# Late index queries placed directly behind the first key/value products, and the second half's norm written columns first

## The chip, the cores and the metric

The kernel runs on one core of a Trainium2 chip. The metric is device time in microseconds (us) of one execution, as the median of several runs. A core has five engines with a queue of their own each: PE (matrix products and transposes, results in PSUM), DVE (vector work), ACT (scalar functions, copies, casts), POOL (a second elementwise engine) and SP (issues most DMAs). Each engine runs its queue in order and waits where an operand or a buffer isn't ready.

## The reference, cut to what matters

Two layers run over 528 tokens (16 meta tokens and 512 of the sequence), each with

```python
h = rms_norm(x, norm_g)
proj = jnp.einsum('btd,de->bte', h, w_in)
q, k, v, gate_a, u_b, gate_b, q_idx, k_idx, w_idx, merge = jnp.split(proj, ...)
k = apply_rope(rms_norm(k, kn_g), cos, sin)
q_idx = apply_rope(q_idx.reshape(B, T, N_IDX_HEADS, IDX_DIM), cos_h, sin_h)
k_idx = apply_rope(k_idx, cos, sin)
...
s = jnp.einsum('bqhd,bkd->bqhk', q_idx, k_idx)
score = jnp.einsum('bqhk,bqh->bqk', jax.nn.relu(s), w_idx * idx_scale)
_, sel = lax.top_k(score, k_top)
```

The index scores choose which keys each query attends to. Attention over the chosen keys, a pooling branch, two gates and an output product follow; they are not touched here.

## The kernel before, in words

**Tokens and halves.** The tokens lie in five groups t = 0 to 4 (`TOK`): the 16 meta tokens, then four of 128. The first half of the columns holds t = 0, 1, 2 (272 tokens), the second half t = 3, 4 (256). The normed input is kept three times: `nf` (float32), and split into `hhi` and `hlo`, a high and a low part for products in a faster format.

**Who orders what.** PE and DVE run in exactly the order in which the program writes their instructions. ACT, POOL and SP are ordered by the framework's scheduler; `tc.issue_after(ins)` keeps instructions of such an engine behind `ins`. `later(fn, n)` puts a piece of work behind the n-th next call of `group_done()`; each product group (some 3 us of PE) ends in one `group_done()`, which runs what is due, then one piece of weight preparation (`prep_one`), then takes one or two steps from `fill`, the list of index score steps. Below, "#n" is the n-th `group_done()` of a layer.

**The start of a layer** (lines 1172 to 1225) is where the change lies. On PE, in this order:
- `plain_trio`: keys, values and index keys of t = 1, 2 and, by columns, t = 0, from float32 `nf` and the raw weights. In layer 1 it has `stats(1)` inside, which sums the squares of the second half; POOL then makes `msq`, the factors of its norm. In layer 0 `x_half(1)` follows. #1 runs `kv_post` of t = 1 and 2 (rotary reads of PSUM on DVE).
- layer 1 only: `hooks[1]`, the second half's norm, `norm_half(1, 1, mm, LAG3)`.
- `late_queries(0)` (line 710): index queries of the 64 last tokens of t = 1, 32 small products into one bank `d`. Its `post`, which reads the bank on DVE with the rotary tables (`late_tab`), is due at #2.
- layer 0 only: the second half's norm, `norm_half(0, 1, rstd, LAG1)`. Then #2.
- index queries of t = 2 (`index_queries`, "q2", weights in split form); #3.
- keys and values of t = 3 ("k3") and of t = 4 ("k4") from `nf` of the second half, `plain_group`; #4 and #5.
- index queries of t = 3 ("q3") and 4 ("q4"); #6 and #7. Then the second set of weights: late queries, q2, q3, q4; #8 to #11.

`norm_half` (line 473) spreads the factors over the partitions by PE transposes into `rb`, then runs over k = 0 to 7: DVE writes column k of `nf` (a scalar_tensor_tensor that reads `rb` in PSUM), ACT copies it to `hhi`, and the low part `hlo` of column k - lag is taken (a tensor_sub of two SBUF operands, on POOL for k = 1, 3, 5, 7, on DVE for the others). The lag is 2 in layer 0 and 3 in layer 1, so columns and low parts alternate on DVE.

**PSUM.** Product groups use banks `d`, of which there are three: the trio takes two, the late queries the third, q2, k3 and k4 the same three again. A group can start when the DVE reads of the group three before it have ended. Transposes and scores use the four banks `a`.

**Behind the groups.** `kv_post` goes on with `second` (scaling), `third` (split into `ks`) and `trans` (PE transposes to the key tables `KK` and `KI`, copied by ACT): for t = 1, 2 at #2, #3, #5; for t = 0, whose sum ends at #2, at #3, #4, #6. The late queries: cast, subtraction, transposes and the entry of their two score steps into `fill` at #3, #5, #6 and #7. The score steps multiply with `KI[:, :, :144]`, that is with the index keys of t = 0 and 1.

**Rows turned out, layer 1.** `turn_rows(k)` transposes a tile of the layer's input on DVE into `turned` (four slots) and writes it to DRAM at the next `group_done()` in four SP DMAs (`kept<-turned`, line 1160). The eight calls stand in the first eight groups from #2 on. `turned` shares its memory (tag "D") with `silb`, which is written first behind the first gate product (`dense`, some 6 us behind q4 of the second set).

**Weights.** `w_prep_enqueue(True, after)` behind #5 enqueues the second index weights: two ACT casts (`w<-raw`, line 189) and two DVE subtractions. In layer 0 the casts are kept behind the norm's last `hhi` copy (`halved`); in layer 1 `after` is None. The next chunk (chunk 3) gets its low parts by an accumulating DMA from POOL (line 204).

Of the kernel before, what the change touches and what calls it, by code (L numbers as in the profile page):

```python
# [16 lines left out]
KT = D // 128  # L17
# [15 lines left out]
CAP = 1.5  # L33
W0 = 16
LAG0 = 2
LAG1 = 2
LAG2 = 3
LAG3 = 3
FI = 6
QN = 2  # L40
R_IDX = 3
# [47 lines left out]
def tile_block(ctx: ExitStack, tc: tile.TileContext, x, meta, w_in, pool_w, w_a, w_b, w_out, rows, hgain, c_tab, out):  # L89
# [43 lines left out]
    raws, ready = {}, {}  # L133
# [179 lines left out]
    def later(fn, n=2):  # L313
        pend.append((count[0] + n, fn))
# [159 lines left out]
    def norm_half(l, hf, rstd, lag=1, pool=(1, 3, 5, 7)):  # L474
        a, n = (0, HB) if hf == 0 else (HB, T - HB)
        rb = bank("a")
        for t in ((0, 1, 2) if hf == 0 else (3, 4)):
            s, m = TOK[t]
            pe.transpose(rb[:, s - a:s - a + m], rstd[:m, t:t + 1].to_broadcast([m, 128]), ident[:m, :m])
        if hf == 0:  # L480
            NF[0] = [one.tile([128, 4, T], F32, tag=tag, name="nf") for tag in ("Ahi", "Alo")]
        nf = [NF[0][k // 4][:, k % 4, a:a + n] for k in range(KT)]
        for k in range(KT + lag):
            if k < KT:
                t = nf[k]
                dve.scalar_tensor_tensor(t, RES[0][:, k, a:a + n], parT[:, l * 8 + k:l * 8 + k + 1], rb[:, :n],
                                         op0=OP.mult, op1=OP.mult)
                end = act.copy(hhi[:, k, a:a + n], t)
            if k >= lag:
                j = k - lag  # L490
                (gp if j in pool else dve).tensor_sub(hlo[:, j, a:a + n], nf[j], f(hhi[:, j, a:a + n]))
        return end.ins
# [214 lines left out]
        act.activation(X0["abs"], wp[:, :4], AF.Abs, scale=IDX_SCALE)  # L707
        act.activation(X0["sign"], wp[:, :4], AF.Sign, scale=-1.0)

    def late_queries(g, raw):  # L710
        ps = bank("d")
        for k in range(KT):
            for a in range(2):
                pe.matmul(ps[64 * a:64 * a + 64, :128], NF[0][k // 4][:, k % 4, 80:144],
                          raw[k // 4][:, k % 4, 128 * a:128 * a + 128], start=k == 0, stop=k == KT - 1,
                          skip_group_check=True)

        def post():
            p3 = ps[:, :128].rearrange("p (h d) -> p h d", h=2)
            t1 = tmp.tile([128, HB], F32, tag="tt", name="t1", bufs=6)  # L720
            t2 = tmp.tile([128, HB], F32, tag="tt", name="t2", bufs=6)
            v1 = t1[:, :128].rearrange("p (h d) -> p h d", h=2)
            dve.tensor_tensor(v1, p3, ctab0[:, None, :].to_broadcast([128, 2, 64]), op=OP.mult)
            dve.tensor_tensor(t2[:, :128].rearrange("p (h a d) -> p h a d", h=2, a=2), swapped(ps[:, :128], 2),
                              stab0.rearrange("p (a d) -> p a d", a=2)[:, None, :, :].to_broadcast([128, 2, 2, 32]),
                              op=OP.mult)
            gp.tensor_tensor(t1[:, :128], t1[:, :128], t2[:, :128], op=OP.add)
            qs = tmp.tile([128, 2, 128], F32R, tag="P", name="qs", bufs=PB)
            dst = tmp.tile([128, 2, 128], F32R, tag="B", name="q0", bufs=8)

            def trans():
                tp = bank("a", F32R)
                for b in range(2):
                    pe.transpose(tp[:, b * 128:b * 128 + 128], qs[:, b, :], identr)
                act.copy(dst, f(tp)[:, :256].rearrange("p (h c) -> p h c", h=2))
            later(lambda: act.copy(qs[:, :, 0:64], v1), 1)
            later(lambda: dve.tensor_sub(qs[:, :, 64:128], v1, f(qs[:, :, 0:64])), QI)
            later(trans, QI + 1)
            later(lambda: fill.append(late_scores(g, dst)), FI - 1)
        later(post, 1)  # L740

    def late_scores(g, q):
        n = NK[0]
# [397 lines left out]
    hooks = {0: lambda: None}  # L1141

    for l in range(2):
# [38 lines left out]
            later(lambda t=t, ps=pss[t]: kv_post(l, t, ps), 1)  # L1182
        later(lambda ps=pss[0]: meta_sum(ps, KV, lambda total: kv_post(l, 0, total)), 1)
        group_done()
        if l:
            hooks[1]()
        turns = deque(range(KT))

        def late_chunk(g, c):
            late_queries(g, raws.pop(c))  # L1190
            w_load()

        for what, t in (("q", 1), ("q", 2), ("k", 3), ("k", 4), ("q", 3), ("q", 4)):
            if what == "k":
                ps = plain_group(t, raws[kv])
                later(lambda t=t, ps=ps: kv_post(l, t, ps), 1)
            elif t == 1:
                late_chunk(0, early_raw)
                if l == 0:
                    halved = norm_half(0, 1, rstd, LAG1)  # L1200
            else:
                index_queries(t, 0, w)
            if l and turns:
                turn_rows(turns.popleft())
            group_done()
            if (what, t) == ("k", 4):
                del raws[kv]
                w_load()
                w_prep_enqueue(True, None if l else halved)
        w = chunk()  # L1210
        for t in range(1, 5):
            if t == 1:
# [185 lines left out]
        if l == 0:  # L1398
# [42 lines left out]
            for hs in (halves[:1], halves[1:]):  # L1441
# [5 lines left out]
                if hs[0][0] == 0:  # L1447
                    later(lambda: stats(0), 1)
                    later(lambda: norm_half(1, 0, mm, LAG2), 2)
            hooks = {0: lambda: stats(1), 1: lambda: norm_half(1, 1, mm, LAG3)}  # L1450
        else:
            for c in range(4):
                w = chunk()
# [66 lines left out]
```

## Time and profile before

| | |
|---|---|
| runs | 751.58, 752.74, 753.07 us; median 752.74 |
| profiled execution | 751.12 us, its span 749.3 us |
| granted TensorE clock | 0.998 |
| PE busy | 98% of the span |
| DVE, ACT, POOL busy | 76%, 62%, 28% |

The span runs from the first to the last instruction of the core; the execution's time is 1.8 us longer. A row of the timeline gives start, length, engine, line, operation, output and inputs, the number of instructions merged, and in brackets how long the engine sat idle before and what ended that. Nearly all PE and DVE instructions carry line 61, a helper, so they are told apart by their tiles. Layer 0 spans some 10 to 384 us, layer 1 the rest; the stretches in question are 18 to 45 us and 385 to 440 us.

### The profile page before, as it was taken

Reading aid. Unit: us, or ns where it says so; the run is one execution under the profiler, and the core shown is the slowest. Engines: PE = TensorE matmul, PEld = TensorE weight load, DVE = VectorE, ACT = ScalarE, POOL = GpSimd, SP = SyncE. Lnnn points to the kernel's source line nnn. Section 1 sums busy time; section 2 is a strip of 40 time slices with the busy share of each in tenths; the row PEclk is TensorE's granted clock in tenths of the full one; section 3 lists DMA queues with packets and bytes.
Section 4 is the critical chain, followed back from the end, with each engine's and each line's share of the span. In section 5 each row is a group of like instructions: output and inputs, shape, how many; then the busy total and the mean of one; then the engine's idle time right before and its main releaser. Section 6 shows DMA issues by size and latency. Waiting matters only on the chain.

```text
span 749.3 us, 15627 instructions
## 1 busy us (share of the span) xinstructions
PE 733.2 (98%) x5906; PEld 699.5 (93%) x5906; DVE 566.1 (76%) x1420; ACT 461.9 (62%) x1027; POOL 210.7 (28%) x280
## 2 busy tenths in 40 slices
PE   8999999999999999999998999999999999999998
PEld 7899999999999999999997988988989999999998
DVE  6866897789898776794448859987998878778631
ACT  5678745648878795543235688455587887774310
POOL 2651065243012010063345411761511110104200
PEclk9999999999999999999999999999999999999999
DMA  8658676776132222543404989768822332237321
GB/s 265 220 140 205 147 156 169 169 185 156 29 85 57 58 58 83 178 156 95 113 1 101 199 171 261 184 141 201 203 76 57 87 85 57 57 103 236 106 77 44
DMA packets 89003, 96.87 MB, mean 129 GB/s; under 512 B 20656, under 2 KB 75728, under 8 KB 88928
## 3 DMA queue, kind: packets, MB, share of 16 engines
q1 hardware_dynamic: 82800, 74.76, 33.6%
q0 software_dynamic: 5760, 20.97, 15.4%
q8 instruction: 46, 0.75, 0.4%
q14 instruction: 29, 0.24, 0.1%
q10 hardware_dynamic: 368, 0.15, 0.1%
HBM read 66.41 MB, written 8.49 MB: 100 GB/s over the span
## 4 chain that ended last, share of the span: by engine, by line
PE 81%; DVE 8%; ACT 8%; issue 2%; POOL 1%; DMA 1%; ACTq 0%; DVEq 0%; SPq 0%
PE d L61 69%; PE a L61 9%; PE v L61 3%; DVE w L61 2%; ACT lt L829 2%; ACT w L238 1%; ACT lt L840 1%; DVE raw L61 1%; DVE lt L61 1%; DVE c L61 1%; ACT pt L856 1%; DMA raw<-in_w_in_dram 1%; DVE alo L61 1%; DVE s L61 1%; DVE hlo L61 0%
## 5 line engine op out<-in xcount | busy, mean ns | idle before, releaser
L61 PE MATMUL d<-hhi,w 128*128 128x256 f32 (+3 forms) x1408 | 287.0, 296 | 0.2
L61 PEld LDWEIGHTS d<-hhi,w 128*128 128x128 f32 x1408 | 225.8, 188 | 5.9 <-DVE c L61 0.7
L61 PE MATMUL d<-hlo,w 128*128 128x256 f32 (+3 forms) x704 | 193.4, 294 | 0.0
L61 PEld LDWEIGHTS d<-hlo,w 128*128 128x128 f32 x704 | 132.8, 189 | 2.6 <-issue 0.2
L61 DVE TENSOR_TENSOR w<-raw,w 128x512 fp32r<-128x512 f32 (+1 forms) x128 | 107.8, 852 | 2.4 <-ACT w L238 2.3
L61 PE MATMUL d<-w,hhi 128*128 128x256 f32 x704 | 109.1, 284 | 0.0
L61 PEld LDWEIGHTS d<-w,hhi 128*128 128x128 f32 x704 | 96.0, 188 | 4.1 <-issue 1.8
L61 PE MATMUL d<-hsum,w 128*128 128x264 f32 (+1 forms) x576 | 76.5, 285 | 0.0
L841 POOL TENSOR_SCALAR pm<-lt,rs 128x16 f32<-128x16 f32 x48 | 27.8, 592 | 171.0 <-DVE rs L61 163.6
L61 PEld LDWEIGHTS d<-hsum,w 128*128 128x128 f32 x576 | 71.6, 188 | 0.8 <-ACT lt L840 0.3
L61 PE MATMUL d<-w,hlo 128*128 128x256 f32 x352 | 67.3, 281 | 0.0
L204 POOL DMA_DIRECT2D w<-raw x40 | 36.1, 916 | 100.2 <-ACT w L203 86.8
L238 ACT CAST w<-raw 128x512 fp32r<-128x512 f32 x96 | 56.9, 624 | 1.8 <-DVE raw L61 1.7
L1384 POOL TENSOR_TENSOR hlo<-ta,hhi 128x256 fp32r<-128x256 f32 (+1 forms) x28 | 28.2, 1020 | 96.5 <-PE d L61 83.2
L61 DVE MATCH_REPLACE8 sc<-m,sc 128x400 f32<-128x400 f32 (+2 forms) x100 | 54.3, 548 | 0.0
L61 DVE MAX8 m<-sc 128x8 f32<-128x400 f32 (+2 forms) x100 | 52.7, 556 | 0.8
L61 PEld LDWEIGHTS d<-w,hlo 128*128 128x128 f32 x352 | 52.7, 188 | 0.0
L829 ACT ACTIVATE lt<-lt,mn,NR 128x144 f32<-128x144 f32 (+3 forms) x64 | 42.4, 666 | 13.9 <-DVE mn L61 13.8
L61 PE MATMUL d<-mhi,w 128*128 128x272 f32 (+2 forms) x192 | 47.6, 328 | 0.0
L189 ACT CAST w<-raw 128x1024 fp32r<-128x1024 f32 x32 | 33.5, 1046 | 21.7 <-PE d L61 19.3
L203 ACT ACTIVATE w<-raw 128x1024 fp32r<-128x1024 f32 x40 | 41.5, 1059 | 7.0 <-PE d L61 7.0
L208 ACT CAST w<-raw 128x1024 fp32r<-128x1024 f32 x40 | 41.5, 1050 | 0.0
(224 smaller groups left out, 1386.6 us busy)
## 6 DMA issues: line engine op xcount, KB each, us to landing
raw<-in_w_in_dram SPq DMA_DIRECT2D x72, 512.0 KB, 4.3
w<-raw POOLq DMA_DIRECT2D x40, 512.0 KB, 6.0
raw<-in_w_out_dram SPq DMA_DIRECT2D x16, 512.0 KB, 3.5
raw<-in_w_branch_b_dram SPq DMA_DIRECT2D x8, 512.0 KB, 4.6
raw<-in_w_branch_a_dram SPq DMA_DIRECT2D x8, 512.0 KB, 4.0
kept<-res SPq DMA_DIRECT2D x8, 264.0 KB, 5.5
res<-kept SPq DMA_DIRECT2D x8, 264.0 KB, 5.7
xt<-in_x_dram SPq DMA_DIRECT2D x4, 512.0 KB, 6.1
```

The source lines that it names most:

```text
L61: return fn(*a, **k)
L189: act.copy(his[s], raws[c][s])
L203: act.activation(t, raws[c][s], AF.Copy, scale=-1.0)
L204: gp.dma_start(t, raws[c][s], accum_op=OP.add)
L208: act.copy(t, raws[c][s])
L238: act.copy(t[:, 0], blk[src[n]])
L829: act.activation(L[hh][:, :n], L[hh][:, :n], AF.Exp, scale=NR[:, i, h:h + 1], bias=mn[:, hh:hh + 1], accum_out=sm[:, hh:hh + 1])
L840: act.activation(L[hh][:, 16:n], L[hh][:, 16:n], AF.Copy, scale=rs[:, hh:hh + 1])
L841: (gp if j < 3 else dve).tensor_scalar(pms[i][:, 2 * j + hh, :], L[hh][:, 0:16], rs[:, hh:hh + 1], None, op0=OP.mult)
L856: act.copy(pt[:, :2 * len(bs)], tp[:, :256 * len(bs)].rearrange("p (a c) -> p a c", c=128))
L1384: pool_end = gp.tensor_sub(hlo[:, j, a:a + n], d, f(hhi[:, j, a:a + n]))
```

## The change

`late_queries` gets a flag `now`: its `post` then runs at once instead of at #2, so that all its later steps come one group earlier (cast #2, subtraction #4, transposes #5, entry into `fill` #6). In both layers the late queries stand directly behind #1, their rotary reads behind them, and the second half's norm behind those; the norm's lag is KT = 8, so that all eight columns come ahead of all eight low parts. In layer 1 the high casts of the second index weights are now kept behind the norm's last copy, too. `turn_rows` begins at k3: four calls at k3, k4, q3 and q4, four in the second set (#8 to #11).

```diff
-LAG1 = 2
...
-LAG3 = 3
...
-    def late_queries(g, raw):
+    def late_queries(g, raw, now):
...
-        later(post, 1)
+        if now:
+            post()
+        else:
+            later(post, 1)
...
-        if l:
-            hooks[1]()
         turns = deque(range(KT))

-        def late_chunk(g, c):
-            late_queries(g, raws.pop(c))
+        def late_chunk(g, c, now=False):
+            late_queries(g, raws.pop(c), now)
             w_load()

-        for what, t in (("q", 1), ("q", 2), ("k", 3), ("k", 4), ("q", 3), ("q", 4)):
+        late_chunk(0, early_raw, True)
+        halved = norm_half(0, 1, rstd, KT) if l == 0 else hooks[1]()
+        group_done()
+        for what, t in (("q", 2), ("k", 3), ("k", 4), ("q", 3), ("q", 4)):
             if what == "k":
                 ps = plain_group(t, raws[kv])
                 later(lambda t=t, ps=ps: kv_post(l, t, ps), 1)
-            elif t == 1:
-                late_chunk(0, early_raw)
-                if l == 0:
-                    halved = norm_half(0, 1, rstd, LAG1)
             else:
                 index_queries(t, 0, w)
-            if l and turns:
+            if l and t > 2:
                 turn_rows(turns.popleft())
             group_done()
             if (what, t) == ("k", 4):
                 del raws[kv]
                 w_load()
-                w_prep_enqueue(True, None if l else halved)
+                w_prep_enqueue(True, halved)
...
-            hooks = {0: lambda: stats(1), 1: lambda: norm_half(1, 1, mm, LAG3)}
+            hooks = {0: lambda: stats(1), 1: lambda: norm_half(1, 1, mm, KT)}
```

## The prediction, as written before the result

> **What bounds the kernel now.** I read the page first, then the waits of PE.
>
> ```profile
> span 749.3 us, 15627 instructions
> PE 733.2 (98%) x5906; PEld 699.5 (93%) x5906; DVE 566.1 (76%) x1420; ACT 461.9 (62%) x1027; POOL 210.7 (28%) x280
> ```
>
> ```profile
> PE d L61 <- DVE t L61: 3.5, 2, 2.2
> ...
> PE a L61 <- POOL msq L466: 1.1, 1, 1.1
> ```
>
> PE is busy 733.2 of 749.3 us, so 16 us is all that a reordering could win, and the change removes no product. What counts is which idle stretches of PE it touches. The second view names them (total, times, longest): two waits of PE for DVE's `t`, 3.5 us together, and one for POOL's `msq`. The timeline shows where they lie. First layer 0:
>
> ```profile
> 20.96 1.97 PE L61 MATMUL d<-raw,nf 128*64 128x128 f32 x32
> ...
> 23.33 1.26 DVE L61 SCALAR_TENSOR_TENSOR nf<-res,parT,a 128x256 f32<-128x256 f32 x3 [0.81 <-PE a L61]
> ...
> 25.43 1.43 POOL L491 TENSOR_TENSOR hlo<-nf,hhi 128x256 fp32r<-128x256 f32 x2
> ...
> 25.75 1.40 DVE L61 TENSOR_TENSOR hlo<-nf,hhi 128x256 fp32r<-128x256 f32 x1
> 26.82 2.87 PE L61 MATMUL d<-raw,nf 128*128 128x200 f32 x16
> ...
> 28.58 0.56 DVE L61 TENSOR_TENSOR hlo<-nf,hhi 128x256 fp32r<-128x256 f32 x1
> ...
> 30.39 0.47 DVE L61 TENSOR_TENSOR t<-d,late_tab 128x128 f32<-128x128 f32 x2
> ...
> 31.01 2.94 PE L61 MATMUL d<-raw,nf 128*128 128x200 f32 x16 [1.32 <-DVE t L61]
> ```
>
> The late queries (20.96, 32 products) end at 22.93. Their rotary reads run only at 30.39 to 30.86, behind the whole norm (23.33 to 29.14) on DVE. k3 (26.82) ends at 29.69; k4 needs the bank that the late queries still hold, and starts at 31.01, 1.32 us later. Layer 1 in the same view:
>
> ```profile
> 392.89 0.88 PE L61 MATMUL v<-raw,nf 128*32 128x200 f32 x16
> ...
> 394.92 0.43 PE L61 MATMUL a<-consts,msq 128*128 128x128 f32 x2 [1.14 <-POOL msq L466]
> ...
> 395.28 1.97 PE L61 MATMUL d<-raw,nf 128*64 128x128 f32 x32
> ...
> 397.69 1.21 PE L61 MATMUL d<-w,hhi 128*128 128x256 f32 x8
> ...
> 400.63 2.87 PE L61 MATMUL d<-raw,nf 128*128 128x200 f32 x16
> 400.96 1.05 ACT L189 CAST w<-raw 128x1024 fp32r<-128x1024 f32 x1 [1.95 <-DMA raw<-in_w_in_dram]
> ...
> 402.96 0.75 DVE L61 TENSOR_TENSOR hlo<-nf,hhi 128x256 fp32r<-128x256 f32 x1 [0.19 <-ACT hhi L488]
> ...
> 405.08 0.47 DVE L61 TENSOR_TENSOR t<-d,late_tab 128x128 f32<-128x128 f32 x2
> 405.69 2.94 PE L61 MATMUL d<-raw,nf 128*128 128x200 f32 x16 [2.19 <-DVE t L61]
> ```
>
> Two waits here. PE ends the trio at 393.77 and idles 1.14 us, because the next thing in its order is the transposes of `msq`, still in the making on POOL; the late queries, which need none of it, stand behind. Later k4 waits 2.19 us for the same rotary reads (405.08). ACT also stood 1.95 us for a weight load in the midst of the norm's copies, and so held up the low parts.
>
> **The change, part by part.** *Rotary reads ahead of the norm.* In layer 0 they can run at about 23.0, when their bank is full; DVE sat idle 0.81 us before the columns there, so they cost nothing: they end at 23.5 and the columns start 0.1 to 0.2 us later. k4's bank is then free 6 us before 29.69, and the wait of 1.32 us goes. In layer 1 it is the same: the reads follow the late queries, and the 2.19 us go.
>
> *Late queries ahead of the norm's transposes, layer 1.* They start at 393.77 and end at 395.74, by when `msq` has been there since about 394.9. The idle 1.14 us goes; q2 begins at 396.55 instead of 397.69. Sum of the waits: 1.32 + 1.14 + 2.19 = 4.65 us. What it costs: in layer 1 the columns begin at about 396.3.
>
> *Columns ahead of low parts.* One column takes 0.42 us (three in 1.26). Eight end 3.4 us after their start: at 26.9 in layer 0 and 399.7 in layer 1. k3 reads them one by one from 26.82 and from 400.63 - 1.14 = 399.5, the last of them 2.5 us after its start, so it never catches up. The price is that the low parts run in one block. A low part takes DVE some 0.42 us undisturbed (an estimate: the 0.56 row is the shortest quoted, the column of the same shape takes 0.42), but the one at 25.75 took 1.40 us while POOL was at its own two, 1.43 us (0.72 each). Four take 1.7 us if nothing disturbs; with two of POOL's in the way, as the copies' pace suggests, 1.7 + 1.4 = 3.1. The norm then ends at 28.6 to 30.0 in layer 0 (29.14 before) and at 401.4 to 402.8 in layer 1 (402.96 + 0.75 = 403.71 before, where DVE waited for the held-up copies). [...]
>
> *What is late next: DVE behind the norm.* The late transposes move from #6 to #5, directly behind the key transposes, and their subtraction to #4.
>
> ```profile
> 32.93 0.40 DVE L61 TENSOR_TENSOR ks<-t,ks 16x256 fp32r<-16x256 f32 x1
> ...
> 33.65 0.94 PE L61 MATMUL a<-identr,ks 128*128 128x128 f32 x8
> ```
>
> ```profile
> 408.33 0.94 PE L61 MATMUL a<-identr,ks 128*128 128x128 f32 x8
> 408.41 0.53 DVE L61 TENSOR_TENSOR ks<-t,ks 16x256 fp32r<-16x256 f32 x1
> ...
> 411.52 0.27 DVE L61 TENSOR_TENSOR qs<-t,qs 128x128 fp32r<-128x128 f32 x1
> ```
>
> The subtraction (0.27) takes its place directly ahead of the meta keys' split (32.93, 408.41). In layer 0 that place is 3.79 us behind the norm's end, less 0.4 for the reads that are gone; with its own 0.27 it ends 3.7 us behind the norm: at 32.3 to 33.7. PE wants it when the key transposes are through: 33.65 - 1.32 + 0.9 = 33.2. In layer 1 the place was 4.7 us behind the norm, now without two of its three row transposes (0.7 each) and without the reads: 4.7 - 1.4 - 0.4 + 0.3 = 3.2, so 404.6 to 406.0 against 408.33 - 3.33 + 0.9 = 405.9. PE stalls 0 to 0.5 us in layer 0 and 0 to 0.1 in layer 1; I take 0.3 for both together. The transposes themselves only change groups, and the split of t = 1, 2, which the key transposes need, ends about a microsecond earlier in this chain.
>
> *Score steps into `fill` at #6.* This adds a wait. At #6 the meta keys (t = 0) are transposed, and the score steps, which come right behind, read them from `KI`.
>
> ```profile
> 37.91 0.48 PE L61 MATMUL a<-identr,ks 16*128 16x16 f32 x4
> ...
> 38.32 0.36 PE L61 MATMUL a<-identr,qs 128*128 128x128 f32 x2
> ...
> 38.50 0.19 ACT L620 CAST KI<-a 128x32 fp32r<-128x32 f32 x1
> ```
>
> PE could go on 0.41 us after the start of these transposes (38.32); ACT's copy to `KI` ends 0.78 us after it (38.69). Before, the late transposes and all of q4 lay between. Now PE stands 0.37 us, and up to 0.15 more for the handover (the reads that end at 30.86 let k4 start at 31.01): 0.45 in each layer, 0.9 together. Queued behind the waiting step on PE is q4, so all of it is path. If ACT had the `KI` copy of t = 0 earlier than I think, it would be 0.
>
> *`turn_rows` later, casts behind the norm, layer 1.* Both free DVE and ACT where they are short (counted above). Their price is the time of the last rows, under the rivals. The casts are wanted only at #7, and come about when they came before (400.96), since the load they need also starts 1.5 us earlier.
>
> Sum: 4.65 - 0.9 - 0.3 = 3.45 us. Behind that PE has no other wait before the attention stage that the change would fill, and all later work on the other engines starts from PE's products, so I let the shift stand to the end. The profiled execution (751.12) would go to 747.7, its span to 745.9. It lies 1.6 us under the median of the runs, 752.74; taken from that, 749.3.
>
> **The rivals.** *The low parts exclude each other fully.* If all four of POOL's low parts fall in DVE's way, not two, the norm ends 1.4 us later than my late ends, at 31.4 and 404.2, and the subtractions at 35.1 and 407.4: PE stalls 1.9 and 1.5 us there. Gain 4.65 - 0.9 - 3.4 = 0.3, time 752.4. Against it: POOL starts its low parts when `hhi` of column 1 is copied, some 2 us before DVE has ended the columns. [...] I give 0.1.
>
> *ACT sets the pace later in layer 1.* The chain of waits runs there over ACT:
>
> ```profile
> 444.65 0.37 ACT r L750
> 445.02 0.38 ACT r L683
> ...
> 450.61 0.77 ACT r L683 x2
> ```
>
> If ACT can't begin this earlier, layer 1's part is waited back: gain 1.32 - 0.45 - 0.2 = 0.7, time 752.0. Against it: these copies belong to scores that PE makes, and shift with them. I give 0.12.
>
> *The last turned rows hold up `silb`: slower.* Its place is the first write of `silb`, which waits until all of `turned` has been read.
>
> ```profile
> 421.46 0.70 DVE L61 STREAM_TRANSPOSE turned<-res 128x512 f32<-128x512 f32 x1
> ...
> 422.62 7.43 SPq L1160 DMA_DIRECT2D kept<-turned  x8
> ...
> 438.88 0.69 DVE L61 SCALAR_TENSOR_TENSOR silb<-th,d 128x512 f32<-128x512 f32 x1 [0.55 <-ACT th L1242]
> ...
> 441.55 0.42 DVE L61 TENSOR_TENSOR qs<-t,qs 128x256 fp32r<-128x256 f32 x1
> ```
>
> ```profile
> 446.57 0.47 PE L61 MATMUL a<-identr,qs 128*128 128x128 f32 x4
> ```
>
> ```profile
> L1160 SPq DMA_DIRECT2D kept<-turned x4: 487/1134/1522, 425.6 to 428.5; - x4
> ...
> DMA to landing us min/median/max: 5.5/6.4/7.8
> ```
>
> Before, eight writes stood behind the load of the next chunk and the last was issued at 428.5, landed by 436.3, 2.6 us before `silb` at 438.88. Now sixteen stand there, from 422.62 - 2.8 = 419.8 on. At 0.93 us each (7.43 for eight) the last is issued at 434.7 and lands at 440.2 to 442.5; `silb` wants to be written at 438.88 - 2.8 = 436.1, so DVE stands some 4 to 6 us. PE feels that only through the subtraction behind it (441.55 to 441.97), whose transposes come at 446.57: 4.6 us of room. So the loss is 0 to 1.8 us at this pace, and 0 if the writes not directly behind a load go faster, as I take it. At 1.13 us each (the median of the last four) and 7.8 to land it is 445.7: DVE stands 9.6, PE 5.0, and 751.12 becomes 752.7, the median 754.3. It turns slower from landings behind 444.2 on. I give 0.06.
>
> *It doesn't do what it says*: the scheduler of ACT puts the norm's copies or the meta keys' behind other work, and DVE waits for them: 752.7 again. I give 0.02, since the added order of the casts takes away the wait that the trace shows.
>
> **How the numbers follow.** The forecast has 0.70; its own range is from 0.37 + 0.7 more stall (gain 2.6, 750.1) to no stall at all (gain 4.65, 748.1). A measurement can tell about 0.2%, 1.5 us, from no change. Faster: 0.70, half of the port rival (between 0.3 and the forecast lie its milder cases) and a few hundredths of ACT's: 0.78. Same: the rest of those two and the last rival, 0.15. Slower: 0.07. For 8 in 10 the range goes from 748.0 past the forecast's own end to the milder cases of the port and of `silb`, 751.5.
>
> **What would show it.** In the changed profile: no PE wait for DVE's `t` ahead of k4 in either layer, no wait for `msq`; eight columns in a row on DVE, the reads of `late_tab` ahead of them; a new PE wait of about 0.4 us for ACT's `KI` ahead of the late score step; at most 0.5 us ahead of the late transposes. It is wrong if a new PE wait for DVE's `qs` or `ks` of over 1 us stands there, if `silb` waits for a DMA and PE behind it, or if PE's idle time grows in the attention stage by what the start gave.

## The result and the profile after

Over six runs each, the changed kernel takes 747.88 us (747.07 to 748.90) against 751.72 us (751.26 to 753.07): a ratio of 0.9943, with an interval of 0.9928 to 0.9958. The forecast was faster, 749.3 us with a range from 748.0 to 751.5; the sign was right, the three waits went as forecast, and the time lies 0.1 us below the range. The two profiled executions, 751.12 and 748.78 us, differ by 2.34 us only; the medians differ by 3.84. Both numbers have to be explained. Line numbers of the changed kernel are two lower up to the start of a layer (helper L59 for L61, `KI` copy L618 for L620, `qi` copy L664 for L666); the row writes are L1161 for L1160.

The page of the changed kernel, and the waits of PE in it (total, times, longest):

```profile
span 747.0 us, 15616 instructions
...
PE 733.1 (98%) x5906; PEld 699.7 (94%) x5906; DVE 565.6 (76%) x1420; ACT 462.5 (62%) x1027; POOL 210.8 (28%) x280
```

```profile
PE a L59 <- ACT qi L664: 1.6, 2, 1.0
...
PE a L59 <- ACT KI L618: 0.7, 2, 0.4
```

PE's busy time is unchanged (733.1 against 733.2), so the whole difference is idle time. The waits for DVE's `t` (3.5 us) and for `msq` (1.1) are gone. Two new ones stand there: the one for `KI` that was forecast, and one for ACT's `qi` that was not. The timeline of the start, layer 0:

```profile
21.23 1.97 PE L59 MATMUL d<-raw,nf 128*64 128x128 f32 x32
...
27.09 5.58 PE L59 MATMUL d<-raw,nf 128*128 128x200 f32 x32
...
33.13 0.33 PE L59 MATMUL a<-identr,qs 128*128 128x128 f32 x2
...
37.64 0.67 PE L59 MATMUL a<-KI,q 128*128 128x144 f32 x4 [0.36 <-ACT KI L618]
```

```profile
23.25 0.59 DVE L59 TENSOR_TENSOR t<-d,late_tab 128x128 f32<-128x128 f32 x2 [0.46 <-PE d L59]
23.76 3.21 DVE L59 SCALAR_TENSOR_TENSOR nf<-res,parT,a 128x256 f32<-128x256 f32 x8
26.89 2.52 DVE L59 TENSOR_TENSOR hlo<-nf,hhi 128x256 fp32r<-128x256 f32 x4
...
32.16 0.27 DVE L59 TENSOR_TENSOR qs<-t,qs 128x128 fp32r<-128x128 f32 x1
```

k3 and k4 have become one unbroken row of 32 products (27.09), 5.58 us long where the two took 2.87 and 2.94 apart. DVE reads the rotary values at 23.25, then writes eight columns in a row, then its four low parts. The late transposes (33.13) wait for nothing. The one wait left in this stretch is 0.36 us, ahead of the late score step. In layer 1 the same:

```profile
392.86 1.97 PE L59 MATMUL d<-raw,nf 128*64 128x128 f32 x32
394.76 0.43 PE L59 MATMUL a<-consts,msq 128*128 128x128 f32 x2
...
398.70 5.58 PE L59 MATMUL d<-raw,nf 128*128 128x200 f32 x32
...
404.75 0.34 PE L59 MATMUL a<-identr,qs 128*128 128x128 f32 x2
...
409.26 0.45 PE L59 MATMUL a<-KI,q 128*128 128x144 f32 x2 [0.36 <-ACT KI L618]
```

To see where the gain stays, I matched PE's products into the banks `d` of the two traces by their number and took the start of each, counted from the late queries of layer 0. The changed kernel is 1.12 us ahead from the start of layer 0 to its end, 4.22 us ahead when layer 1 reaches its first gate product (the forecast had 3.45), and then 2.6 us ahead until the end. So 1.6 us is given back within 25 us. That place in the timeline of the changed kernel, PE first, then SP's queue, ACT and DVE:

```profile
435.91 0.51 PE L59 MATMUL a<-KI,qi 128*128 128x256 f32 x2 [0.55 <-ACT qi L664]
...
448.30 0.70 PE L59 MATMUL a<-sc,consts 128*64 128x144 f32 x4 [1.04 <-ACT qi L664]
```

```profile
418.59 15.62 SPq L1161 DMA_DIRECT2D kept<-turned  x16
434.32 2.49 SPq L143 DMA_DIRECT2D raw<-in_w_in_dram  x2
```

```profile
433.81 1.08 ACT L201 ACTIVATE w<-raw 128x1024 fp32r<-128x1024 f32 x1
...
446.23 1.06 ACT L201 ACTIVATE w<-raw 128x1024 fp32r<-128x1024 f32 x1 [1.85 <-DMA raw<-in_w_in_dram]
447.19 0.58 ACT L1240 ACTIVATE th<-d 128x512 f32<-128x512 f32 x1
447.67 0.58 ACT L664 CAST qi<-a 128x512 fp32r<-128x512 f32 x1
```

```profile
439.52 0.69 DVE L59 SCALAR_TENSOR_TENSOR silb<-th,d 128x512 f32<-128x512 f32 x1 [4.76 <-ACT w L206]
```

SP issues sixteen row writes in one stretch, and the two weight loads only behind them, at 434.32. In the trace of before the rows were through earlier, and the loads went out at 432.12, although PE was 4 us further back there:

```profile
432.12 4.30 SPq L145 DMA_DIRECT2D raw<-in_w_in_dram  x2
```

ACT stands 1.85 us for the loaded weights, with `th` and `qi` behind that in its order, and PE waits 1.04 us for `qi`. At the first wait, of 0.55 us, ACT isn't idle: it makes a cast of weights that are there (433.81) directly ahead of `th` and `qi`. DVE's stand at `silb` (4.76 us) cost PE nothing. Its row names a cast of ACT that ended at that time, but the last row write, issued at 433.70, landed only at 439.43, too.

### The profile page after: what moved, and what is told of

The parts are those of the page before. It is cut to its first block, busy times and chain, and to the rows that moved or that the text cites. A ratio compares the mean times of both kernels' runs of the same rounds, so it can differ in the third digit from the quotient of the medians.

```text
span 747.0 us, 15616 instructions
## 1 busy us (share of the span) xinstructions
PE 733.1 (98%) x5906; PEld 699.7 (94%) x5906; DVE 565.6 (76%) x1420; ACT 462.5 (62%) x1027; POOL 210.8 (28%) x280
## 4 chain that ended last, share of the span: by engine, by line
PE 82%; DVE 7%; ACT 7%; DMA 1%; issue 1%; POOL 0%; ACTq 0%; DVEq 0%
PE d L59 69%; PE a L59 9%; PE v L59 3%; DVE w L59 2%; ACT lt L830 2%; DMA raw<-in_w_in_dram 1%; ACT w L236 1%; ACT lt L841 1%; DVE raw L59 1%; DVE lt L59 1%; DVE c L59 1%; ACT pt L857 1%; DVE alo L59 1%; DVE s L59 1%; DVE sc L59 0%
## 5 line engine op out<-in xcount | busy, mean ns | idle before, releaser
L59 PE MATMUL d<-hhi,w 128*128 128x256 f32 (+3 forms) x1408 | 287.1, 296 | 0.2
L59 PEld LDWEIGHTS d<-hhi,w 128*128 128x128 f32 x1408 | 225.9, 188 | 5.9 <-DVE c L59 0.7
L59 PE MATMUL d<-hlo,w 128*128 128x256 f32 (+3 forms) x704 | 193.5, 294 | 0.0
L59 PEld LDWEIGHTS d<-hlo,w 128*128 128x128 f32 x704 | 132.9, 189 | 2.5 <-issue 0.2
L59 DVE TENSOR_TENSOR w<-raw,w 128x512 fp32r<-128x512 f32 (+1 forms) x128 | 107.8, 851 | 2.4 <-ACT w L236 2.3
L59 PE MATMUL d<-w,hhi 128*128 128x256 f32 x704 | 109.1, 284 | 0.0
L59 PEld LDWEIGHTS d<-w,hhi 128*128 128x128 f32 x704 | 96.0, 188 | 4.1 <-issue 1.8
L59 PE MATMUL d<-hsum,w 128*128 128x264 f32 (+1 forms) x576 | 76.5, 286 | 0.0
L59 PEld LDWEIGHTS d<-hsum,w 128*128 128x128 f32 x576 | 71.6, 188 | 0.8 <-ACT lt L841 0.3
L59 PE MATMUL d<-w,hlo 128*128 128x256 f32 x352 | 67.6, 281 | 0.0
L59 DVE MATCH_REPLACE8 sc<-m,sc 128x400 f32<-128x400 f32 (+2 forms) x100 | 54.3, 548 | 0.0
L59 DVE MAX8 m<-sc 128x8 f32<-128x400 f32 (+2 forms) x100 | 52.6, 556 | 0.8
L59 PEld LDWEIGHTS d<-w,hlo 128*128 128x128 f32 x352 | 52.8, 188 | 0.0
L59 PE MATMUL d<-mhi,w 128*128 128x272 f32 (+2 forms) x192 | 47.7, 328 | 0.0
```

The lines of the kernel that those rows point to most:

```text
L59: return fn(*a, **k)
```

## The experiments

The theory at the start: the gain at the gates is lost because the row writes, which the change puts later, hold the load back on SP, and with it ACT's `qi`. Its rivals: ACT is the pace there whatever SP does; or one of the other parts (score steps, norm order, casts) costs what is missing. A second theory came up on the way, for the difference between traces and medians: PE's waits in the kernel before draw stretches at half the granted clock. "Ahead" below is the shift of PE's products against the first trace of before, as above. Intervals are of the ratio to the kernel before, on the same chip in the same batch. Most of them overlap with that of the change, so what tells the versions apart is the shift, in one trace of each.

**Two rows at each of q3 and q4, so that all eight are out two groups earlier.**

```diff
             if l and t > 2:
                 turn_rows(turns.popleft())
+                if what == "q":
+                    turn_rows(turns.popleft())
```

> The changed kernel, but at q3 and q4 of layer 1 two rows are turned out each, so that the last of the eight calls stands at q2 of the second set, as before the change. Theory A: in the changed kernel the sixteen row writes fill SP's queue from 418.59 to 434.2, the load of the next weight chunk goes out behind them (434.32 instead of 432.12, though PE is 3.6 us earlier), lands at 446.2, ACT stands 1.85 us for it and PE 1.04 us for the cast of qi behind that; so here that PE wait goes and the kernel is 1.0 to 1.6 us faster than the changed one, ratio to before about 0.9925, and silb no longer waits on DVE. Rival B: the loss between the first and the second gate product is ACT's order and not the rows; then it stays, and the ratio is that of the changed kernel, 0.9943.

747.03 us, ratio 0.9933 [0.9914, 0.9951]. Only eight writes are left ahead of the load, `silb` hardly waits, and the long wait for `qi` is gone. The short one is 0.2 us: the cast that stood ahead of `th` and `qi` stands behind them here, at 434.26. These are SP, DVE and PE of this kernel:

```profile
420.31 11.82 SPq L1161 DMA_DIRECT2D kept<-turned  x8
432.23 1.40 SPq L143 DMA_DIRECT2D raw<-in_w_in_dram  x2
```

```profile
434.34 0.69 DVE L59 SCALAR_TENSOR_TENSOR silb<-th,d 128x512 f32<-128x512 f32 x1 [1.06 <-DMA kept<-turned]
```

```profile
PE a L59 <- ACT qi L664: 0.2, 1, 0.2
```

PE arrives at the gates 3.3 us ahead and leaves them 3.6 us ahead: nothing is given back. In its trace layer 0, whose code is that of the change, is only 0.5 us ahead in place of 1.12, since it loses 0.54 us some 39 us behind the late queries, where the timeline shows no wait; the cause is open, and it hides part of the gain in the total.

**Rows from #2 on, one in each group, as before.**

```diff
         halved = norm_half(0, 1, rstd, KT) if l == 0 else hooks[1]()
+        if l:
+            turn_rows(turns.popleft())
         group_done()
...
-            if l and t > 2:
+            if l and turns:
                 turn_rows(turns.popleft())
```

> The changed kernel, but the rows are turned out from #2 on, one in each of the first eight groups, as before the change. Theory A: the PE wait of 1.04 us behind the gate product goes (last row two groups earlier), but two row transposes of 0.7 us stand on DVE ahead of the late queries' subtraction, which ended at 404.6 with PE wanting it at 404.75: a new PE wait of about 1.2 us ahead of the late transposes in layer 1, so about the time of the changed kernel, ratio 0.994. Rival B (rows not at fault in the gate stage): only the new wait shows, 1.2 us slower than the changed kernel, ratio 0.996.

747.69 us, 0.9941 [0.9922, 0.9960], so no other than the change. Both sides of the move show: nothing is lost at the gates (2.70 us ahead, then 2.68), but 0.85 us earlier on. The row transposes stand between the norm and the subtraction, and the late transposes wait:

```profile
404.36 0.37 PE L59 MATMUL a<-identr,qs 128*128 128x128 f32 x2 [0.85 <-DVE qs L59]
```

So the later rows do buy what the prediction wanted of them at the start of the layer, and pay for it at its gates. (Here, too, layer 0 loses some 0.45 us without a visible cause.)

**The score steps at #7 again.**

```diff
-            later(lambda: fill.append(late_scores(g, dst)), FI - 1)
+            later(lambda: fill.append(late_scores(g, dst)), FI if now else FI - 1)
```

> The changed kernel, but the two early score steps enter the list at #7 as before the change, so that q4 stands between the meta keys' transposes and the steps that read them. Theory A: the PE waits for ACT's KI copy (0.36 us and the restart, about 0.45 in each layer) go: 0.7 to 0.9 us faster than the changed kernel, ratio about 0.9932. Rival B: the waits are only moved, since the steps then meet qi's transposes at #7; then within 0.2 us of the changed kernel.

747.17 us, 0.9932 [0.9911, 0.9954]. Both waits for `KI` are gone, and PE is 1.53 us ahead in layer 0 (1.12 with the change), so this wait costs 0.4 us in each layer. But the 5.03 us that PE is ahead at the gates shrink to 2.64: the waits at the gates take back all of it, mostly that for `qi`. In the view of PE's waits:

```profile
PE a L59 <- ACT qi L664: 1.8, 2, 1.3
```

**The rotary reads at #2 again**, with the late queries left in their new place; all later steps of the late queries come one group later, too, the score steps at #7.

```diff
-        late_chunk(0, early_raw, True)
+        late_chunk(0, early_raw)
```

> The changed kernel, but the rotary reads of the early late queries run at #2 again, behind the norm on DVE (the late queries themselves stay ahead). Theory A: the reads are what held k4's bank: k4 waits again in both layers, by about 1.2 us in layer 0 (reads end some 6.9 us later) and about 1 to 2 us in layer 1, where the norm's DVE part now ends earlier; the KI wait of 0.45 per layer goes, since the steps enter at #7: 1.5 to 2.5 us slower than the changed kernel, ratio 0.9965. Rival B: the order columns first alone frees DVE enough that the reads come in time: within 0.5 us of the changed kernel or faster by the two KI waits.

748.64 us, 0.9950 [0.9931, 0.9968]. The wait for DVE's `t` ahead of k4 is back, 1.0 us in each layer (the view of PE's waits):

```profile
PE d L59 <- DVE t L59: 2.0, 2, 1.0
```

PE is 0.31 us ahead in layer 0 and 2.47 at the gates, 1.75 less than with the change, and ends 2.34 ahead. The early reads, with the `KI` waits that they bring, are thus worth 1.75 us where they act, of which the gates let through 0.24 (2.58 against 2.34 at the end).

**The old lags of the norm** (2 and 3), the rest as in the change.

```diff
-        halved = norm_half(0, 1, rstd, KT) if l == 0 else hooks[1]()
+        halved = norm_half(0, 1, rstd, 2) if l == 0 else hooks[1]()
...
-            hooks = {0: lambda: stats(1), 1: lambda: norm_half(1, 1, mm, KT)}
+            hooks = {0: lambda: stats(1), 1: lambda: norm_half(1, 1, mm, 3)}
```

> The changed kernel, but columns and low parts of the second half's norm alternate as before (lag 2 in layer 0, 3 in layer 1). Theory A: columns first are needed so that k3 and k4 don't meet late columns: in layer 0 the last column would end at about 28.9 instead of 27.0, before k3 reads it (29.6), so nothing changes there; in layer 1 at about 401 to 402 instead of 398.9, where k3 reads the last at 401.2: a PE wait of 0 to 1 us. Loss 0 to 1 us against the changed kernel. Rival B: alternating lets POOL and DVE get out of each other's way, the norm ends earlier, and nothing is lost.

747.12 us, 0.9941 [0.9918, 0.9964]; 1.12 us ahead in layer 0, 3.77 at the gates, 2.7 at the end. The columns-first order is worth 0 in layer 0 and 0.45 in layer 1, and nothing of that at the end.

**The casts of layer 1 not held back.**

```diff
-                w_prep_enqueue(True, halved)
+                w_prep_enqueue(True, None if l else halved)
```

> The changed kernel, but in layer 1 the high casts of the second index weights aren't kept behind the norm's last copy. Theory A: ACT takes a cast in the midst of the norm's copies and stands for its weight load (1.95 us before the change; the load lands at 400.5 here), the low parts come about 1 to 2 us later, and PE waits 0.5 to 1.5 us ahead of the late transposes in layer 1. Rival B: with all columns ahead, the copies are through (399.2) before the load lands, and nothing changes.

748.64 us, 0.9954 [0.9937, 0.9971]. ACT puts one cast among the norm's copies; the timeline of ACT and two rows of PE:

```profile
396.20 1.19 ACT L486 CAST hhi<-nf 128x256 fp32r<-128x256 f32 x3
397.67 1.05 ACT L187 CAST w<-raw 128x1024 fp32r<-128x1024 f32 x1 [0.28 <-DMA raw<-in_w_in_dram]
398.62 1.63 ACT L486 CAST hhi<-nf 128x256 fp32r<-128x256 f32 x5
```

```profile
405.40 0.36 PE L59 MATMUL a<-identr,qs 128*128 128x128 f32 x2 [0.44 <-DVE qs L59]
...
444.40 0.51 PE L59 MATMUL a<-identr,qs 128*128 128x128 f32 x4 [0.48 <-DVE qs L59]
```

PE is 3.56 us ahead at the gates, 0.66 less than with the casts kept behind; the order added to them is worth that. At the end it is 2.6 ahead again. It is not the load that takes it back here: PE has the first wait for `qi` (0.55 us) but not the second, and in its place waits 0.48 us at 444.40 for the subtraction behind `silb`, at which DVE stands 5.78 us. That is the route which the prediction had looked at.

These runs answer the question of the rivals. With the rows as the change has them, kernels that reach the gates 3.6, 3.8, 4.2 and 5.0 us ahead all end 2.6 to 2.7 us ahead. The last part of the loss goes by either route: by `qi` in the change, by `silb` without the added order of the casts, by both with the score steps at #7 (1.27 and 0.31 us). Only where the rows move is nothing lost there.

**Both: rows paired and score steps at #7.**

> The changed kernel with two rows each at q3 and q4 of layer 1, and with the early score steps at #7. Both parts won by themselves, in the traces from the start of layer 0's queries to the end: 0.94 us for the rows (2.58 to 3.52 against before), 0.41 us in layer 0 and 0.64 us in layer 1 up to the gate product for the scores. Theory A (they are independent): 2.58 + 0.94 + 0.41 + 0.4 = 4.3 us of gain against before in the trace, time about 746 at the same granted clock. Rival B: the score steps at #7 put back what they won when ACT is free of the load wait; then 3.5 us as with the rows alone.

745.64 us, 0.9913 [0.9895, 0.9931], the best of all versions. PE is 1.54 us ahead in layer 0, 5.04 at the gates and 5.29 at the end, where the two parts by themselves made 4.3. SP and the wait for `qi` in it:

```profile
418.82 12.64 SPq L1161 DMA_DIRECT2D kept<-turned  x8
431.57 1.01 SPq L143 DMA_DIRECT2D raw<-in_w_in_dram  x2
```

```profile
432.80 0.50 PE L59 MATMUL a<-KI,qi 128*128 128x256 f32 x2 [0.18 <-ACT qi L664]
```

ACT can therefore go faster there than it does in the changed kernel; with the rows out earlier it is not the pace.

**The load ahead of the last two rows.** The change as it is, but the writes of the last two rows are kept behind the load on SP. If the load is what `qi` waits for, that wait goes, and `silb`, which waits for the rows, gets the delay in its place.

```diff
+    last_load = [None]
...
-            nc.sync.dma_start(raws[c][s][:, :, o:o + src.shape[2]], src[:, s * kt // 2:(s + 1) * kt // 2, :])
+            last_load[0] = nc.sync.dma_start(raws[c][s][:, :, o:o + src.shape[2]],
+                                             src[:, s * kt // 2:(s + 1) * kt // 2, :]).ins
...
             def leave():
-                for a in range(4):
-                    dma(rows_[:, :, k * 128 + 32 * a:k * 128 + 32 * a + 32],
-                        t[32 * a:32 * a + 32].rearrange("p (b j) -> p b j", j=32))
-            later(leave, 1)
+                with tc.issue_after(last_load[0]) if k >= 6 else nullcontext():
+                    for a in range(4):
+                        dma(rows_[:, :, k * 128 + 32 * a:k * 128 + 32 * a + 32],
+                            t[32 * a:32 * a + 32].rearrange("p (b j) -> p b j", j=32))
+            later(leave, 9 - k if k >= 6 else 1)
```

> The changed kernel, but on SP the writes of the last two rows of layer 1 stand behind the next chunk's load instead of ahead of it. Theory A (the load behind the rows is what costs PE): the load goes out at about 430 instead of 434.3, ACT no longer stands for it (1.85 us), and the PE wait of 1.04 us for the cast of qi goes; silb's DVE wait grows from 4.8 to some 6 to 9 us, which costs PE nothing up to some 5 us and the rest beyond: net between 1.1 us faster and 2.5 us slower than the changed kernel, with the wait's releaser changed from ACT behind a DMA to DVE. Rival B (the DMA engines' load, not the order, makes the load late): it goes out earlier, lands as late as 446, and the same PE wait of 1 us stands.

753.02 us, 1.0016 [1.0003, 1.0029]: a little slower than the kernel before, and further behind the change than the 2.5 us that the expectation allowed. Up to the gates it runs as the change does (3.77 us ahead behind the first wait). SP, DVE and PE there:

```profile
428.67 1.75 SPq L145 DMA_DIRECT2D raw<-in_w_in_dram  x2
430.50 10.03 SPq L1165 DMA_DIRECT2D kept<-turned  x8
```

```profile
443.70 0.69 DVE L59 SCALAR_TENSOR_TENSOR silb<-th,d 128x512 f32<-128x512 f32 x1 [8.98 <-DMA kept<-turned]
```

```profile
446.93 0.72 PE L59 MATMUL a<-identr,qs 128*128 128x128 f32 x4 [3.68 <-DVE qs L59]
```

```profile
PE a L59 <- ACT qi L667: 0.6, 1, 0.6
```

The loads go out at 428.67, 5.65 us earlier than with the change, and ACT takes both casts of the loaded weights at 440.82 without a wait. The second wait for `qi` (1.04 us) is gone; only the first, of 0.55, is left, so that one is not due to the load. That the second is gone proves little by itself, since PE comes there 3.7 us later. But in the change `qi` ended at 448.25 and PE wanted it at 447.26; without ACT's 1.85 us it would have ended at 446.4. So the late load was the cause of the longer wait; the kernels with the rows paired agree, where PE comes there no later than in the change and does not wait. The price is the prediction's slower rival in full: `silb` waits 8.98 us for the last rows, and PE waits 3.68 us for the subtraction queued behind `silb` on DVE. PE falls from 3.77 us ahead to 2.59 behind, 6.4 us, which is more than the wait. The windows view of this kernel shows the rest (length, busy us and count of PE, PEld, DVE, ACT, POOL, then the granted clock):

```profile
442.23:445.65 3.42, 1.02 (x5) 0.49 (x3) 1.91 (x3) 2.88 (x4) 1.68 (x2) 1.00 0.92 245
445.65:449.06 3.41, 2.13 (x10) 2.07 (x11) 3.17 (x8) 2.80 (x6) 0.00 (x0) 0.50 1.07 238
449.06:452.47 3.41, 3.41 (x10) 2.82 (x9) 3.31 (x7) 0.79 (x2) 0.00 (x0) 0.50 1.03 229
452.47:455.88 3.41, 3.41 (x17) 2.56 (x16) 1.44 (x6) 1.11 (x3) 0.00 (x0) 1.00 0.76 225
```

Behind a stretch in which PE was busy 1.02 of 3.42 us, the granted clock is 0.5 for two stretches of 3.41 us. In them a product of 128x512 starts every 0.43 us (from 448.48 on), behind them every 0.23 us (from 452.53 on). PE was busy 2.13 + 3.41 = 5.54 us in them, of which about half, 2.8 us, is by this pace my estimate of the loss. 3.68 + 2.8 = 6.5, against 6.4 found.

**The kernel before once more**, with a profile of a run at a mean granted clock of 0.995 (the first profile had 0.998).

> The kernel before, again. Of its eleven timed executions of the last comparison seven had a granted clock of 0.995 and 752.7 to 753.6 us, one had 1.0 and 749.09. Theory A: the wide spread of the kernel before is a granted clock of one half in single stretches of 3.41 us (one of them stood at 11.8 us of its first profile), and its PE waits of layer 1 (1.14 and 2.19 us) call one more of them, of some 1.7 us; a profile at 0.995 shows it behind 394 or 405 us. Rival B: all such stretches lie in the first 25 us, and the changed kernels drew fewer by chance.

752.41 us, 1.0003 [0.9987, 1.0018]; the profiled run took 753.2 us, its span 751.4. Its waits are those of the first profile but one: k4 in layer 1 waits 2.68 us instead of 2.19, and runs 4.37 us instead of 2.94. Its row in the timeline:

```profile
406.38 4.37 PE L61 MATMUL d<-raw,nf 128*128 128x200 f32 x16 [2.68 <-DVE t L61]
```

The windows of this run, then the same stretch of the first profile of before:

```profile
404.33:407.74 3.41, 1.36 (x8) 1.39 (x9) 3.41 (x14) 1.44 (x4) 1.83 (x3) 1.00 0.40 64
407.74:411.15 3.41, 3.41 (x16) 3.31 (x14) 3.04 (x10) 1.11 (x6) 1.58 (x3) 0.50 0.77 120
```

```profile
404.33:407.74 3.41, 2.05 (x12) 2.08 (x13) 3.41 (x14) 1.41 (x6) 1.17 (x2) 1.00 0.56 89
407.74:411.15 3.41, 3.41 (x29) 3.24 (x28) 3.41 (x15) 2.29 (x13) 2.80 (x6) 1.00 0.76 120
```

In this run PE was busy 1.36 us of one stretch, and the next runs at half clock; in the first it was busy 2.05, and the clock stays. From there on this run is 2.1 us behind the first, about half of 3.41 us and the 0.49 us by which the wait is longer. Of the runs of before whose clock is listed, 22 of 61 were at 0.995, all within 752.66 and 753.64 us; three more took as long at 0.999 or 1.0. Of the 48 runs of the change and of its variants above, without the one that puts the load first, one was.

**The kernel before with the wait filled.** Twenty products of 256 columns, whose result nothing reads, stand ahead of k4 in layer 1, where PE would wait.

```diff
             if what == "k":
+                if l and t == 4:
+                    pad = bank("a")
+                    for _ in range(20):
+                        pe.matmul(pad[:, :256], identr, hhi[:, 0, 0:256], start=True, stop=True)
                 ps = plain_group(t, raws[kv])
```

> The kernel before, with twenty products of 256 columns whose result nobody reads on PE ahead of k4 of layer 1, some 2.2 us of work in place of the wait of 2.19 us; all other waits stay. Theory A (the granted clock falls to one half for 3.41 us behind a stretch in which PE did little, and that is why the kernel before has executions at 0.995 and 752.7 to 753.6 us): no execution at 0.995 and none over 752.3 us is left, the others stay at 749.5 to 752.1; the median falls by 0.5 to 1 us although PE has more to do. Rival B (the half clock in layer 1 has nothing to do with the wait): a third to two thirds of the executions stay at 0.995.

750.15 us, 0.9985 [0.9972, 0.9998]. In the trace nothing moves (0.1 us): the products lie in the wait, and k4 starts behind them where it started before.

```profile
403.44 2.67 PE L61 MATMUL a<-hhi,identr 128*128 128x256 f32 x20
405.99 2.94 PE L61 MATMUL d<-raw,nf 128*128 128x200 f32 x16
```

Yet none of its 12 runs was at 0.995, against 5 of 23 of the kernel before in the same batch. (One took 753.39 us at 0.999, and two of before in this batch took as long at 1.0; the runs don't show why.) Work without any use makes the kernel no slower. In its profile PE is busy for all of 404.33 to 407.74, where it was busy 1.36 and 2.05 us in the two profiles of before, and the clock behind it is 1.00. That the products do away with the half clock there is likely but not sure: none of 12 beside 5 of 23 would come by chance about one time in ten. How much of the 1.5 us between the medians is due to that is less sure: 8 of its 12 runs were at 0.999 or 1.0, against 6 of 23 of before's, so by the clock more of them also lacked the half-clock stretch that other runs have at about 12 us, which these products cannot reach.

## Why the prediction was right and where it was wrong

**Right: the three waits.** 1.32, 1.14 and 2.19 us are gone, and the reads, columns and low parts run in the order forecast. The block of low parts took DVE 2.52 and 2.37 us, within the 1.7 to 3.1 forecast. The norm ends at 29.41 in layer 0, within its window, and at 401.16 in layer 1, 0.2 us ahead of it, since the columns begin at 395.65 there and not at 396.3. The first rival, which the prediction also calls the port rival, did not come: it needed all of POOL's low parts in DVE's way.

```profile
25.46 3.00 POOL L489 TENSOR_TENSOR hlo<-nf,hhi 128x256 fp32r<-128x256 f32 x4
```

POOL starts 1.43 us ahead of DVE's block in layer 0, as the argument against that rival said, so half of its 3.00 us falls beside it. DVE's four took some 0.8 us more than 1.7, about one of POOL's low parts, with an overlap of 1.57 us (26.89 to 28.46). What the two engines share there, no run separates; that it is a port is not shown.

**Right but too dear: the new waits.** The wait for `KI` is 0.36 us in each layer, not 0.45; the kernel with the score steps at #7 gains 0.4. The subtraction ended at 32.43 and 404.58, at the early ends of its windows (32.3 and 404.6), and the late transposes wait for nothing (0.3 taken). And k3 and k4, without a stop between them, are 2.87 + 2.94 - 5.58 = 0.23 us shorter in each layer. So PE is 4.22 us ahead at the gates in place of 3.45. (One sum of the prediction doesn't come out: 0.37 + 0.7 us more of stall would leave 2.4 of the 3.45 us, not 2.6.)

**Wrong: "I let the shift stand to the end".** The step failed at layer 1's gates, where 1.6 of the 4.22 us go. The prediction followed the later row writes along one route, by `silb` and DVE. Of that route it had nearly all: the last write was forecast at 434.7 and goes at 433.7, DVE's stand at 4 to 6 us and is 4.76, PE's loss at 0 and is 0. It left out the other thing that queues behind the rows on SP, the two loads of the next chunk. The last fourteen of SP's sixteen row writes in the changed kernel (duration min/median/max in ns, first and last start):

```profile
L1161 SPq DMA_DIRECT2D kept<-turned x14: 433/556/3700, 419.5 to 433.7; - x14
```

That "all later work starts from PE's products" doesn't hold for this load. In the trace of before SP stood 2.0 us for the DMA that writes `w` and issued it at 432.12; with the change, which had put eight more writes ahead of it, it went out at 434.32, directly behind the last of them. The late issue is only part of the delay. The second load goes out at 435.46 and lands 10.7 us later, at 446.21; with the rows paired it takes 5.8 us (432.78 to 438.53), with the load first 5.9 (430.02 to 435.94). What makes the transfer longer behind the sixteen rows, no run separates.

The ACT rival had the right engine and gave 752.0. For the longer wait its reason was another: ACT stood for a load. The shorter wait, 0.55 of the 1.6 us, is nearer to that rival: ACT works without a break ahead of it, and it stays with the load first. It shrinks or goes only where the rows move, and the order of ACT's casts with them; why the scheduler orders them so is open. Of the prediction's signs of being wrong, the last came in part: PE's idle time grew at the gates by 1.6 us.

**Right: the price of the slower rival.** It did not happen in the change, but the kernel with the load first made it happen: DVE 8.98 us, PE 3.68. The prediction's pair for that case was 9.6 and 5.0, so its room of 4.6 us is 5.3. What it lacked is the half clock behind that wait, by the estimate above another 2.8 us.

**Wrong: the base.** The prediction worked out 747.7 us from the profiled execution, and then put back the 1.6 us by which that run lay under the median of three, 752.74, as if it belonged to the kernel. This step puts the time outside of the range. Over six runs the median of before is 751.72, 1.02 us lower than over three, and the medians differ by 0.39 us more than the 3.45 forecast; together these are the 1.4 us between 749.3 and 747.88. That the 747.7 from the profiled execution comes within 0.2 us of the result is luck, as the next sum shows.

The second profile of before shows what such a difference can be: a half-clock stretch behind k4's wait, by the clock in about a third of the runs. The change takes the wait away, and by the clock nearly all of those stretches with it (one of 48 runs at 0.995). The two steps went opposite ways: 749.3 - 1.6 (the base) + 1.1 (2.34 us between the profiled executions in place of 3.45) gives the profiled execution after, 748.8, and the median after lies 0.9 below that. Of the 1.1, 0.27 is a later start of layer 0's late queries (21.23 against 20.96), ahead of anything that the change moves; without it the gain is 2.6.

Of the 3.84 us between the medians, 2.34 thus lie between two executions that have one half-clock stretch each while PE works, at about 12 us (from 11.83 and 11.85). The other 1.50 are differences of each kernel's runs from its profiled one (0.60 above for before, 0.90 below after). For the change they go along with the granted clock, mostly: 747.07 and 747.08 us at 1.0 and 0.999, three runs of 747.92 to 748.90 at 0.997. For the six runs of before no clock is listed; two of them, 752.74 and 753.07, took as long as the runs at 0.995 do, and the first of these was the prediction's base. That the wait draws the second stretch rests on one profile of before and on the kernel with the load first, and the filled wait bears it out; that it explains the full 1.50 is not shown. Why only some runs have the one at 12 us stays open; all versions have runs at 0.999 or 1.0, without it by the clock.

## What to carry to other kernels

When a step is moved that issues DMAs, list everything behind it on the same queue, loads above all, and follow each to the engine that waits for it; here one route was priced, and the other lost 1.0 us. A gain at the start of a stage can be lost at the next transfer: five versions that were 2.4 to 5.0 us ahead at the gates all ended 2.3 to 2.7 us ahead. And when single runs of one kernel differ by about 2 us, look at the granted clock before you take the difference over to the changed kernel: in the second profile of before a wait of PE that was 0.49 us longer went with 2.1 us.

## What the runs showed of the hardware

In three profiles two half-clock stretches start whole multiples of 3.413 us apart, wherever PE's wait begins. The two of the second profile of before start at 11.79 and 407.73 us, 116 times 3.413 apart, and those of the kernel with the load first at 12.16 and 445.65 (that one 6.82 us long), 127 times; in the first profile of before, the one at 11.83 and a last one, from 749.12 to the end of the span, are 216 times apart. With the time cut into cells at these borders, what differs in layer 1 is how much of PE's wait fell within one cell. Of the wait of 2.68 us, 2.05 us did (PE busy 1.36), and the next cell ran at half clock. Of the wait of 2.19 us, 1.36 us did (busy 2.05; 1.33 by this run's own border, 404.36), and the clock stayed. In the kernel with the load first, a cell with 2.40 us idle was followed by the half clock again. Both waits of the kernel before fall across such a border; in the one profile the half clock followed, and 1.6 us more were lost (2.1 less the 0.49 of the longer wait), in the other it didn't. This doesn't explain the stretch at about 12 us: it follows a cell with PE idle for 1.74 us in the first profile of before and for 1.71 in that of the change, but in the profile of the kernel with the reads at #2 a cell (7.24 to 10.65) in which PE was idle for only 0.67 us.
